# A pool for each operand slot with its splits four products later, the last two projection blocks written straight to the operands, and entry loads ordered by need

## The chip, the cores and the metric

The kernel runs on one core of a Trainium2 chip. The metric is the device time of one execution in microseconds (us), and a lower one is better. Times are the median of several runs; a profiled execution is a run of its own.

## The reference

One decoder layer over 1024 prompt rows and 64 sample rows (8 sequences of 8), 1088 rows in all, with a model width of 1024:

```python
# each layer: x += W_out . concat[NSA heads, multi-scale pooling channels](RMSNorm(x) @ W_in)
#             x += SwiGLU(RMSNorm(x)).   Final RMSNorm.
#   NSA heads: compressed-block, selected-block (top 16 of 64-token blocks) and
#              sliding-window branches, each a masked softmax, combined by gates
#   pooling channels: trailing means over 2/4/8/16 positions, a linear map per group
D_MODEL = 1024; SEQ = 1024; DEC_BATCH = 8; DEC_SEQ = 8; D_FF = 2816

def rms_norm(x, g):
    xf = x.astype(jnp.float32)
    y = xf * lax.rsqrt(jnp.mean(xf * xf, axis=-1, keepdims=True) + EPS)
    return (y * g.astype(jnp.float32)).astype(x.dtype)
```

Everything is fp32. The outputs are the new activations of prompt and sample rows and the rows to be written to the caches.

## The kernel before

**Numbers.** TensorE (PE) multiplies a 32-bit type of shorter mantissa, fp32r. So each fp32 operand is split in two: `hi` is a cast on ScalarE (ACT), `lo` is the rest, a subtraction on VectorE (DVE). A product is then three matmuls: hi·hi, hi·lo, lo·hi. The splits of PE's moving operand are `bhP1`…`bhP3` and `blP1`…`blP3` at the input products and the two halves of `r` at the output products; those of the weights are `sh` and `sl`, made of `wr` (raw) or `ws` (a sum or difference of raw ones).

**Stages.** Projections and compressed keys (to about 400 us of the profile); the attention stream; the entry of the feed-forward part; its input products; its output products; the last group of output products, with the final norm.

**The attention stream** works block by block of 128 queries (8 prompt blocks 0–7; the sample rows count as block 8). Softmax tiles `pcmp`, `psel`, `pwin` of a half block are scaled by 1/sum (`r`) on GpSimd (POOL, L1002), then transposed on PE (L1012) and split (L1020 on ACT, L1021 on DVE). Between its steps, `fill()` runs steps of other work: generators each with a rate, the steps per attention step. `RATES[0]` is the sample group, `RATES[1]` the pooling channels' part of the projection, `RATES[2]` the attention heads' part, `att_out`. What is left of `att_out` when the stream ends is run at the entry.

**att_out** takes blocks in the order 0, 1, 2, 7, 8, 6, 5, 4, 3. For each it loads the rows so far (`xr`) and the attention output (`of2`), splits the latter (`op0`, `op1`), and runs 48 matmuls (L1198–L1200) in two halves, each added to `xr` by DVE (L1272). Behind that, `xr` is stored as `x2t` (L1280), normed to `h`, and `h_out` transposes it (L1303) and multiplies by the norm's weight into `hT` (L1304), which is stored to DRAM: `hdA` for the half of rows of blocks 0, 1, 2, 7 and half of 8; `hdB` in three pieces (160, 128 and 128 rows) for half of 8 with block 6, block 5 and block 4. Block 3 is written to the operand tile itself.

**The entry** (`ffn`, L1478 on) takes four tiles `blk` as operand halves `hA` and `hB` and loads them from `hdA` and `hdB` on SP's queue, between the remaining fills. `combos` builds the seven operands of a Strassen-like scheme (P1, P2, P6, P5, P7, P4, P3, in that order) by subtractions (L1323) and splits (L163, L164). The input products are 22 units of 7 products, each of 24 matmuls of 128x272 (L1396). A product's result (`pq`, in PSUM) is taken out by ACT and DVE in `evict_in` (L1424–L1456), and the weight splits run four products ahead.

**The output products** are 3 groups of 4 units of 7 products of 18 matmuls. Their moving operands lie in DRAM (`td`) in fp32. A pool `ring` of seven tiles `r0`…`r6` holds the seven operands of a group. `load` takes a tile, starts its DMA on POOL's queue (L1565) and issues its split at once (`hilo`, ACT L1568, DVE L1569); the first seven are loaded ahead of the first group, and in the last unit of a group the product that was last to read a slot is followed by the load of that slot for the next group. Results are added to the rows `blk` by DVE (L1468), or copied by ACT in the first group (L1466). Two tiles `la0`, `la1` for the last group are loaded in unit 8.

**Memory.** A pool's memory is taken from what earlier pools freed; the first use of a tile waits for the last users of the memory under its whole pool. The memory under `ring` is that of the `b` tiles of the input products. DMAs on SP's queue are issued in order, and an issue that waits holds those behind it; POOL's queue holds DMA issues and POOL's own instructions alike. A scheduler sets the order on each engine by the order of the program and a priority.

## Time and profile before

| | before |
|---|---|
| median of 3 runs | 1445.89 us (1444.05 to 1447.25) |
| profiled execution | 1448.49 us, its span 1446.7 us |
| mean granted clock of PE | 0.978 |
| busy: PE, DVE, ACT, POOL | 1358.5 (94%), 980.2 (68%), 660.4 (46%), 200.0 (14%) us |
| DMA | 173.79 MB, 120 GB/s in the mean |

A row of the timeline has start and duration in us, then engine, line, operation, output and input tiles and shapes; in square brackets is the idle time of the engine just before, and what ended it. "SPq" and "POOL … DMA" rows are issues of transfers. A row of waits has the total in us, the number and the longest. `x2` or `(x2)` are instructions in the row. Durations of matmuls overlap, so distances between their starts say what each one costs.

### The profile page before, as it was taken

To read this page: it belongs to the slowest core of one execution; us is meant where nothing else is said; L and a number is where in the kernel's file an instruction comes from. 1 tells how busy PE (TensorE), PEld (TensorE's weight loads), DVE (VectorE), ACT (ScalarE), POOL (GpSimd) and SP (SyncE) were. 2 spreads that over 40 slices of the span, in tenths; PEclk is the share of its full clock that TensorE was granted. 3 is DMA by queue.
4 is the path that set the end of the run, shared out by engine and by line. 5 is a ranking of instruction groups with operands and counts; after the bars stand their busy time and mean duration, and the time that the engine had idled before them with its cause. 6 is when DMAs were issued, how large, how long until landed. Compare 5 with 4: busy or idle time off the path is not lost.

```text
span 1446.7 us, 25436 instructions
## 1 busy us (share of the span) xinstructions
PE 1358.5 (94%) x9490; PEld 1263.1 (87%) x9490; DVE 980.2 (68%) x2267; ACT 660.4 (46%) x1502; POOL 200.0 (14%) x338
## 2 busy tenths in 40 slices
PE   7979999899999989996799999999999989999995
PEld 6968999678878878775699999999999979999995
DVE  5655877777776688886866556655655565879557
ACT  7322554776566676764533333333333354434123
POOL 0124223422222232220000000000000010010000
PEclk9989999989999999998899999999999999999998
DMA  7457331534425143325232233333223262535135
GB/s 203 88 156 237 91 103 29 179 118 137 152 94 175 59 137 114 107 83 169 58 121 83 83 106 121 106 114 113 89 77 106 76 222 82 184 125 187 34 107 182
DMA packets 167751, 173.79 MB, mean 120 GB/s; under 512 B 21539, under 2 KB 134787, under 8 KB 166851
## 3 DMA queue, kind: packets, MB, share of 16 engines
q1 hardware_dynamic: 157187, 135.12, 30.5%
q0 software_dynamic: 9392, 35.45, 7.1%
q10 hardware_dynamic: 1048, 1.59, 1.0%
q8 instruction: 75, 1.23, 0.3%
q14 instruction: 49, 0.40, 0.1%
HBM read 113.87 MB, written 58.37 MB: 119 GB/s over the span
## 4 chain that ended last, share of the span: by engine, by line
PE 66%; issue 11%; DVE 9%; DMA 5%; ACT 4%; SPq 3%; POOL 1%; DVEq 0%; POOLq 0%; ACTq 0%
PE pq L1396 36%; PE dp L236 6%; PE tp L1012 3%; SPq L1060 3%; PE O L1036 2%; PE dp L1198 2%; PE dp L1200 2%; PE dp L1199 2%; PE O L1037 2%; PE S L923 2%; PE S L924 1%; DVE pl L1021 1%; DMA r<-td 1%; ACT ph L1020 1%; PE dp L1155 1%
## 5 line engine op out<-in xcount | busy, mean ns | idle before, releaser
L1396 PE MATMUL pq<-bhP,sh 128*128 128x272 f32 x1232 | 357.4, 290 | 11.5 <-ACT sh L163 5.7
L1396 PE MATMUL pq<-blP,sh 128*128 128x272 f32 x1232 | 357.4, 290 | 4.4 <-DVE blP L164 3.1
L1396 PE MATMUL pq<-bhP,sl 128*128 128x272 f32 x1232 | 355.3, 289 | 2.4 <-DVE sl L164 2.4
L1396 PEld LDWEIGHTS pq<-bhP,sh 128*128 128x128 f32 x1232 | 234.2, 190 | 13.3 <-ACT sh L163 6.5
L1396 PEld LDWEIGHTS pq<-blP,sh 128*128 128x128 f32 x1232 | 233.7, 190 | 5.5 <-DVE blP L164 5.5
L1396 PEld LDWEIGHTS pq<-bhP,sl 128*128 128x128 f32 x1232 | 233.6, 190 | 2.9 <-DVE sl L164 2.9
L1396 PE MATMUL pq<-r,sh 128*128 128x272 f32 x1008 | 194.4, 292 | 11.2 <-DVE blk L1468 5.7
L163 ACT CAST sh<-ws 128x512 fp32r<-128x512 f32 (+1 forms) x136 | 78.8, 583 | 217.5 <-PE pq L1396 153.2
L1396 PEld LDWEIGHTS pq<-r,sh 128*128 128x128 f32 x1008 | 160.4, 192 | 12.9 <-DVE blk L1468 6.0
L164 DVE TENSOR_TENSOR sl<-ws,sh 128x512 fp32r<-128x512 f32 (+1 forms) x136 | 86.7, 641 | 124.0 <-ACT sh L163 123.8
L1396 PE MATMUL pq<-r,sl 128*128 128x272 f32 x504 | 145.0, 289 | 0.0
L1021 DVE TENSOR_TENSOR pl<-tp,ph 128x512 fp32r<-128x512 f32 (+8 forms) x168 | 103.7, 622 | 42.6 <-ACT ph L1020 40.9
L163 ACT CAST sh<-wr 128x512 fp32r<-128x512 f32 (+1 forms) x102 | 59.3, 583 | 151.7 <-PE pq L1396 140.9
L1020 ACT CAST ph<-tp 128x512 fp32r<-128x512 f32 (+8 forms) x168 | 88.8, 534 | 67.5 <-PE tp L1012 60.7
L236 PE MATMUL dp<-h1h,whi 128*128 128x384 f32 (+1 forms) x336 | 112.9, 337 | 3.7 <-DVE ue L310 3.7
L236 PE MATMUL dp<-h1l,whi 128*128 128x384 f32 (+1 forms) x336 | 111.8, 333 | 0.0
L236 PE MATMUL dp<-h1h,wlo 128*128 128x384 f32 (+1 forms) x336 | 111.8, 333 | 0.0
L1565 POOL DMA_DIRECT2D r<-td x21 | 16.0, 765 | 631.5 <-PE pq L1396 625.6
L1396 PEld LDWEIGHTS pq<-r,sl 128*128 128x128 f32 x504 | 96.6, 192 | 0.0
L164 DVE TENSOR_TENSOR sl<-wr,sh 128x512 fp32r<-128x512 f32 (+1 forms) x102 | 65.0, 637 | 37.7 <-ACT sh L163 37.6
L1036 PE MATMUL O<-ph,vn 128*128 128x256 f32 x264 | 80.8, 320 | 3.2 <-DVE of L1047 1.7
L1002 POOL TENSOR_SCALAR pwin<-pwin,r 128x640 f32<-128x640 f32 (+4 forms) x64 | 42.7, 670 | 291.7 <-DVE r L995 144.9
(344 smaller groups left out, 3059.0 us busy)
## 6 DMA issues: line engine op xcount, KB each, us to landing
wr<-in_w_ffn_in SPq DMA_DIRECT2D x44, 512.0 KB
td<-blk SPq DMA_DIRECT2D x18, 1088.0 KB
r<-td POOLq DMA_DIRECT2D x21, 816.0 KB, 6.6
wr<-in_w_ffn_out SPq DMA_DIRECT2D x48, 192.0 KB
wraw<-in_w_in SPq DMA_DIRECT2D x14, 512.0 KB
x<-in_x_prompt SPq DMA_DIRECT2D x8, 512.0 KB
qi<-qd SPq DMA_DIRECT2D x8, 512.0 KB
op<-odp SPq DMA_DIRECT2D x16, 256.0 KB
```

The source lines that it names most:

```text
L163: nc.scalar.copy(hi, src)
L164: nc.vector.tensor_tensor(lo, src, hi.bitcast(F32), op=OP.subtract)
L236: nc.tensor.matmul(ps, w[:, k, :], x, start=(k == 0 and j == 0), stop=(k == kt - 1 and j == 2))
L923: nc.tensor.matmul(S[:, c0:c0 + n], q, kh[:, k0:k0 + n], start=True, stop=False)
L1002: nc.gpsimd.tensor_scalar(t, t, r[:, hh, b:b + 1], 1.0, op0=OP.mult, op1=OP.mult)
L1012: nc.tensor.transpose(tp[:kk, 256 * x + 128 * hh:256 * x + 128 * hh + 128], u["P"][hh, b][:, kb * 128:kb * 128 + kk], self.ident)
L1020: nc.scalar.copy(ph[:kk, a:e], tp[:kk, a:e])
L1021: nc.vector.tensor_tensor(pl[:kk, a:e], tp[:kk, a:e], ph[:kk, a:e].bitcast(F32), op=OP.subtract)
L1036: nc.tensor.matmul(o, vv, ph[:kk, cs], start=(2 * t + x == 0), stop=False)
L1037: nc.tensor.matmul(o, vv, pl[:kk, cs], start=False, stop=(2 * t + x == nb - 1))
L1060: reg = nc.sync.value_load(self.ptrow[0:1, 4 * b + kb:4 * b + kb + 1], min_val=0, max_val=39)
L1396: nc.tensor.matmul(ps[:, c, :HQ], w[:, k], x[:, k, cs], start=(fresh and k == 0 and j == 0), stop=(k == kt - 1 and j == 2), skip_group_che ...
```

## The change

It has five parts. `RATES[2]` goes from 1.7 to 1.3. The stores of `x2t`, `hdA` and `hdB` go from SP's to POOL's queue. Blocks 4 and 3 are both written straight to `hB` once that tile exists, so `hdB[2]` is neither stored nor loaded. The entry's loads are put in another order, with the weights' two halves apart. The ring becomes seven pools of one tile, and load and split are separated: the first seven loads are issued ahead of their seven splits, and later a split is issued four products behind its load.

```diff
--- before.py
+++ after.py
@@ -37,7 +37,7 @@
 LATE = (5, 4, 3)
 ORDER = ("P1", "P2", "P6", "P5", "P7", "P4", "P3")
 EPS = 1e-6
-RATES = (0.8, 0.65, 1.7)
+RATES = (0.8, 0.65, 1.3)
 BIG = 1e30
 HUGE = 3e38
 POOLW = (2, 4, 8, 16)
@@ -758,6 +758,7 @@
             self.pst = self.pool("pst2", 2, PSUM, stack=self.psy, side="right")
             self.os = self.ap.tile([128, 4, NS], F32, name="os", bufs=1)
             self.done, self.ofs = [], {8: self.os}
+            self.hB, self.direct = None, []
             self.fills, self.stage, self.hold = [], -1, False
             self.attn_stream()
         self.psx.close()
@@ -1277,7 +1278,7 @@
                     nxt = loads()
             for _ in self.tail:
                 yield
-            nc.sync.dma_start(self.x2t[j][:rows], x[:rows])
+            nc.gpsimd.dma_start(self.x2t[j][:rows], x[:rows])
             h = pool.tile([128, D], F32, name="h")
             ss = pool.tile([128, 1], F32, name="ss", bufs=2)
             v = pool.tile([128, 1], F32, name="v", bufs=2)
@@ -1291,8 +1292,11 @@
 
     def h_out(self, pool, j, rows, h):
         nc = self.nc
-        if j == 3:
-            hts = [b[:, :, 416:544] for b in self.hB]
+        direct = j in (3, 4) and self.hB is not None
+        if direct:
+            p0 = HOME[j][1]
+            hts = [b[:, :, p0:p0 + 128] for b in self.hB]
+            self.direct.append(j)
         else:
             hT = pool.tile([128, 8, 128], F32, name="hT")
             hts = [hT[:, 4 * q:4 * q + 4, :rows] for q in range(2)]
@@ -1307,14 +1311,14 @@
                 yield True
         if j in (0, 1, 2, 7):
             p0 = HOME[j][1]
-            nc.sync.dma_start(self.hdA[:, :, p0:p0 + 128], hT)
+            nc.gpsimd.dma_start(self.hdA[:, :, p0:p0 + 128], hT)
         elif j == 8:
-            nc.sync.dma_start(self.hdA[:, :, 512:544], hT[:, :, 0:32])
-            nc.sync.dma_start(self.hdB[0][:, :, 0:32], hT[:, :, 32:64])
+            nc.gpsimd.dma_start(self.hdA[:, :, 512:544], hT[:, :, 0:32])
+            nc.gpsimd.dma_start(self.hdB[0][:, :, 0:32], hT[:, :, 32:64])
         elif j == 6:
-            nc.sync.dma_start(self.hdB[0][:, :, 32:160], hT)
-        elif j != 3:
-            nc.sync.dma_start(self.hdB[6 - j], hT)
+            nc.gpsimd.dma_start(self.hdB[0][:, :, 32:160], hT)
+        elif not direct:
+            nc.gpsimd.dma_start(self.hdB[6 - j], hT)
         yield True
 
     def combos(self, hA, hB, B, a, e):
@@ -1333,6 +1337,10 @@
         put("P3", B1)
 
     def raw_w(self, u):
+        for _ in self.raw_parts(u):
+            pass
+
+    def raw_parts(self, u):
         if "raw" in u:
             return
         nc, fw, kt = self.nc, self.fw, u["kt"]
@@ -1345,6 +1353,7 @@
                 for e in range(2):
                     nc.sync.dma_start(r[:, e * kt:e * kt + kt], half[e])
             u["raw"].append(r)
+            yield
 
     def side_w(self, u, name):
         nc, fw, kt = self.nc, self.fw, u["kt"]
@@ -1483,14 +1492,23 @@
             B = {}
             ins = [dict(f=f, kt=4, B=B, evict=self.evict_in,
                         src=[(wsrc[:, :, o + 128 * f:o + 128 * f + 128],) for o in (0, FF)]) for f in range(NFF)]
-            for q in range(2):
-                nc.sync.dma_start(hA[q], self.hdA[:, 4 * q:4 * q + 4])
-            self.raw_w(ins[0])
+            pieces = ((0, 160), (160, 128), (288, 128))
+
+            def hb_load(i):
+                p0, n = pieces[i]
+                for q in range(2):
+                    nc.sync.dma_start(hB[q][:, :, p0:p0 + n], self.hdB[i][:, 4 * q:4 * q + 4])
+            w0 = self.raw_parts(ins[0])
+            nc.sync.dma_start(hA[0], self.hdA[:, 0:4])
+            next(w0)
+            nc.sync.dma_start(hA[1], self.hdA[:, 4:8])
+            hb_load(0)
             while self.fills:
                 self.fill()
-            for i, (p0, n) in enumerate(((0, 160), (160, 128), (288, 128))):
-                for q in range(2):
-                    nc.sync.dma_start(hB[q][:, :, p0:p0 + n], self.hdB[i][:, 4 * q:4 * q + 4])
+            hb_load(1)
+            next(w0)
+            if 4 not in self.direct:
+                hb_load(2)
             self.raw_w(ins[1])
             self.wax.close()
             att.close()
@@ -1521,7 +1539,7 @@
             last = self.pool("last", 1, stack=s, side="right")
             lacts = [last.tile([128, 2, 4, HT], F32R, name=f"la{j}") for j in range(2)]
             s4 = ExitStack()
-            ring = self.pool("ring", 1, stack=s4)
+            ring = [self.pool(f"ring{i}", 1, stack=s4) for i in range(7)]
             G, kt = 3, 3
             slot = dict(P1=0, P2=2, P3=3, P5=4, P6=5, P7=6, P4=7)
             Bs = [{} for _ in range(G)]
@@ -1532,11 +1550,13 @@
                 if not todo:
                     return
                 g, q = todo.pop(0)
-                r = ring.tile([128, 2, kt, HT], F32R, name=f"r{nr[0] % 7}")
+                r = ring[nr[0] % 7].tile([128, 2, kt, HT], F32R, name=f"r{nr[0] % 7}")
                 nr[0] += 1
-                Bs[g][q] = self.hilo(r, self.td[g][:, slot[q]].rearrange("k p n -> p k n"))
-            for _ in range(7):
-                load()
+                Bs[g][q] = r[:, 0], r[:, 1]
+                self.raw_in(r, self.td[g][:, slot[q]].rearrange("k p n -> p k n"))
+                return r
+            for r in [load() for _ in range(7)]:
+                self.hilo(r)
             outs = []
             for g in range(G):
                 rows = I["w_ffn_out"][0, 256 * kt * g:256 * kt * (g + 1)].rearrange("(j e p) c -> e p j c", e=2, p=128)
@@ -1544,12 +1564,18 @@
                     outs.append(dict(m=m, g=g, kt=kt, B=Bs[g], evict=self.evict_out,
                                      src=[[rows[e][:, :, 128 * mm:128 * mm + 128] for e in range(2)] for mm in (m, m + 4)]))
 
+            queue = []
+
             def hook(x, q):
-                if x % 4 == 3:
-                    load()
+                queue.append(load() if x % 4 == 3 and todo else None)
                 if x == 8 and q in ("P6", "P7"):
                     j = ("P6", "P7").index(q)
-                    self.hilo(lacts[j], self.tl[4 * j:4 * j + 4].rearrange("q p n -> p q n"), True)
+                    self.raw_in(lacts[j], self.tl[4 * j:4 * j + 4].rearrange("q p n -> p q n"))
+                    queue[-1] = lacts[j]
+                if len(queue) > 4:
+                    r = queue.pop(0)
+                    if r is not None:
+                        self.hilo(r)
             for _ in self.chains(self.sequence(len(outs)), outs, hook):
                 pass
             s4.close()
@@ -1558,16 +1584,15 @@
                     for f in range(4)]
             self.last_group(2 * kt * G, acts, s)
 
-    def hilo(self, r, src, late=False):
+    def raw_in(self, r, src):
+        self.tc.keep_in_program_order(self.nc.gpsimd.dma_start(r[:, 1].bitcast(F32), src))
+
+    def hilo(self, r):
         nc = self.nc
         hi, lo = r[:, 0], r[:, 1]
         raw = lo.bitcast(F32)
-        ld = nc.gpsimd.dma_start(raw, src)
-        if late:
-            self.tc.keep_in_program_order(ld)
         nc.scalar.copy(hi, raw)
         nc.vector.tensor_tensor(lo, raw, hi.bitcast(F32), op=OP.subtract)
-        return hi, lo
 
     def sequence(self, n, entry=False):
         seq = [(0, "P1"), (0, "P2")]
```

On SP's queue at the entry, before (`blk_8576` and `blk_8577` are the two halves of A, `blk_8578` and `blk_8579` those of B; `wr` are weights, `x2t3` block 3's rows):

```order
L1317 DMA hdB128_2_94<-hT_8609 128x1024
L1487 DMA blk_8576<-hdA_91 128x2176
L1487 DMA blk_8577<-hdA_91 128x2176
L1343 DMA wr_8585<-in_w_ffn_in 128x8x128
L1343 DMA wr_8587<-in_w_ffn_in 128x8x128
L1493 DMA blk_8578<-hdB160_0_92 128x4x160
L1280 DMA x2t3_85<-xr_8589 128x1024
L1493 DMA blk_8579<-hdB160_0_92 128x4x160
L1493 DMA blk_8578<-hdB128_1_93 128x4x128
L1493 DMA blk_8579<-hdB128_1_93 128x4x128
```

The same place after:

```order
L1502 DMA blk_8576<-hdA_91 128x2176
L1351 DMA wr_8584<-in_w_ffn_in 128x8x128
L1504 DMA blk_8577<-hdA_91 128x2176
L1500 DMA blk_8578<-hdB160_0_92 128x4x160
L1500 DMA blk_8579<-hdB160_0_92 128x4x160
L1500 DMA blk_8578<-hdB128_1_93 128x4x128
L1500 DMA blk_8579<-hdB128_1_93 128x4x128
L1351 DMA wr_8656<-in_w_ffn_in 128x8x128
```

The store of `hdB128_2` and its two loads are gone, `x2t3` is on another queue, and one weight row stands between the halves of A.

On POOL, the last scalings of the attention stream before:

```order
L1002 TENSOR_SCALAR pwin_8424<-pwin_8424,r_8426 128x512
L1002 TENSOR_SCALAR psel_8416<-psel_8416,r_8426 128x512
L1002 TENSOR_SCALAR pcmp_8396<-pcmp_8396,r_8426 128x32
L1002 TENSOR_SCALAR pwin_8477<-pwin_8477,r_8426 128x512
L1002 TENSOR_SCALAR psel_8460<-psel_8460,r_8426 128x512
L1002 TENSOR_SCALAR pcmp_8453<-pcmp_8453,r_8426 128x32
```

The same place after; `x2t4` is block 4's rows, `hdB128_1` block 5's transposed rows:

```order
L1003 TENSOR_SCALAR pwin_8384<-pwin_8384,r_8386 128x512
L1003 TENSOR_SCALAR psel_8376<-psel_8376,r_8386 128x512
L1003 TENSOR_SCALAR pcmp_8342<-pcmp_8342,r_8386 128x32
L1281 DMA x2t4_86<-xr_8172 128x1024
L1321 DMA hdB128_1_93<-hT_8351 128x1024
L1003 TENSOR_SCALAR pwin_8451<-pwin_8451,r_8386 128x512
L1003 TENSOR_SCALAR psel_8427<-psel_8427,r_8386 128x512
L1003 TENSOR_SCALAR pcmp_8420<-pcmp_8420,r_8386 128x32
```

Two stores stand ahead of the scalings of a half block; the same holds for the blocks ahead of these.

On DVE, the last input unit and the first operands of the output products, before (L1443 is the last step of a result, L1569 the split of an operand):

```order
L1357 TENSOR_TENSOR ws_13962<-ws_13960,wr_13838 128x384
L1443 TENSOR_TENSOR blk_13555<-g2_13651,u2_13702 128x544
L1569 TENSOR_TENSOR r0_13778<-r0_13778 128x1632
L1569 TENSOR_TENSOR r1_13782<-r1_13782 128x1632
L1569 TENSOR_TENSOR r2_13786<-r2_13786 128x1632
L164 TENSOR_TENSOR sl_13865<-wr_13838,sh_13864 128x384
L1468 TENSOR_TENSOR blk_13766<-pq3_13868,blk_13766 128x544
```

The same splits after (L1450 and L1452 are L1441 and L1443 of before, L1595 is L1569):

```order
L1366 TENSOR_TENSOR ws_13836<-ws_13834,wr_13820 128x384
L1595 TENSOR_TENSOR r0_13792<-r0_13792 128x1632
L1450 TENSOR_TENSOR g2_13424<-pq2_13432,g2_13424 128x544
L164 TENSOR_TENSOR sl_13587<-wr_13335,sh_13586 128x512
L1435 TENSOR_TENSOR g1_13521<-pq3_13590,g1_13521 128x544
L1452 TENSOR_TENSOR blk_13551<-g2_13424,u2_13485 128x544
L164 TENSOR_TENSOR sl_13620<-ws_13617,sh_13619 128x512
L1366 TENSOR_TENSOR ws_13846<-wr_13820,wr_13823 128x384
L164 TENSOR_TENSOR sl_13827<-wr_13820,sh_13826 128x384
```

The first split stands ahead of results of the unit before the last; all seven stood behind those of the last unit.

On DVE at the change to the second group, before:

```order
L1569 TENSOR_TENSOR r0_14344<-r0_14344 128x1632
L1468 TENSOR_TENSOR blk_13766<-pq3_14406,blk_13766 128x544
L164 TENSOR_TENSOR sl_14431<-wr_14198,sh_14430 128x384
L164 TENSOR_TENSOR sl_14460<-ws_14457,sh_14459 128x384
L1357 TENSOR_TENSOR ws_14569<-wr_14377,wr_14380 128x384
L164 TENSOR_TENSOR sl_14488<-wr_14377,sh_14487 128x384
L1569 TENSOR_TENSOR r1_14426<-r1_14426 128x1632
L1468 TENSOR_TENSOR blk_13769<-pq2_14324,blk_13769 128x544
L1569 TENSOR_TENSOR r2_14453<-r2_14453 128x1632
L164 TENSOR_TENSOR sl_14519<-ws_14516,sh_14518 128x384
L1569 TENSOR_TENSOR r3_14483<-r3_14483 128x1632
L1468 TENSOR_TENSOR blk_13766<-pq0_14522,blk_13766 128x544
```

The same place after (L1477 is L1468 of before):

```order
L1595 TENSOR_TENSOR r0_14358<-r0_14358 128x1632
L1477 TENSOR_TENSOR blk_13762<-pq3_14418,blk_13762 128x544
L164 TENSOR_TENSOR sl_14441<-wr_14212,sh_14440 128x384
L164 TENSOR_TENSOR sl_14470<-ws_14467,sh_14469 128x384
L1366 TENSOR_TENSOR ws_14577<-wr_14389,wr_14392 128x384
L164 TENSOR_TENSOR sl_14496<-wr_14389,sh_14495 128x384
L1477 TENSOR_TENSOR blk_13765<-pq2_14338,blk_13765 128x544
L164 TENSOR_TENSOR sl_14525<-ws_14522,sh_14524 128x384
L1595 TENSOR_TENSOR r1_14438<-r1_14438 128x1632
L1477 TENSOR_TENSOR blk_13762<-pq0_14528,blk_13762 128x544
L164 TENSOR_TENSOR sl_14551<-ws_14520,sh_14550 128x384
L1595 TENSOR_TENSOR r2_14463<-r2_14463 128x1632
```

The split of `r1` stands two rows further back and that of `r2` three; the additions that stood behind them, or between them, now stand ahead.

## The prediction

> **What bounds the kernel now.** I read the page's head, then busy time by stage, then the waits and the order of time around each stage in which TensorE (PE) is not full. The columns of a window row are us, then busy time of PE, its weight loads, VectorE (DVE), ScalarE (ACT) and GpSimd (POOL), then granted clock, share of the DMA engines and GB/s.
>
> ```profile
> span 1446.7 us, 25436 instructions
> 560.00:620.00 60.00, 59.77 (x351) 47.86 (x352) 48.56 (x176) 40.15 (x109) 12.37 (x20) 1.00 0.35 106
> 620.00:668.00 48.00, 42.19 (x256) 33.82 (x254) 36.89 (x133) 31.49 (x88) 12.38 (x24) 0.96 0.15 56
> 668.00:719.00 51.00, 32.60 (x176) 27.91 (x174) 40.53 (x52) 24.24 (x28) 0.00 (x0) 0.80 0.49 146
> 719.00:1158.00 439.00, 438.66 (x3500) 438.61 (x3501) 252.27 (x374) 151.26 (x253) 0.00 (x0) 1.00 0.32 100
> 1158.00:1190.00 32.00, 25.54 (x182) 24.55 (x181) 22.75 (x25) 18.13 (x22) 5.39 (x7) 0.89 0.66 243
> 1219.00:1286.00 67.00, 64.63 (x511) 64.16 (x510) 50.53 (x75) 27.36 (x41) 5.33 (x7) 1.00 0.42 135
> 1286.00:1373.00 87.00, 83.51 (x647) 82.83 (x646) 65.80 (x95) 30.29 (x42) 6.85 (x9) 0.98 0.41 133
> ```
>
> PE is full in 719–1158 (438.66 of 439), and nothing there can be won by order. It is not full in four places that the change touches: the end of attention, 620–668 (5.81 us idle); the entry of the feed-forward part, 668–719 (18.40 idle, and a clock of 0.80); the passage to the output products, 1158–1190 (6.46 idle, clock 0.89); and the two group changes in 1219–1286 and 1286–1373 (5.86 idle together, part of it beside them). Those are the most that can come out, some 36 us plus the lost clock.
>
> **Attention and the rate 1.7 → 1.3.** A step of the w_out fill issues matmuls like these, six rows from first to last:
>
> ```profile
> 610.37 0.39 PE L1198 MATMUL dp<-rwh,op 128*128 128x512 f32 x1
> ...
> 611.53 0.39 PE L1200 MATMUL dp<-rwh,op 128*128 128x512 f32 x1
> ```
>
> So one is 1.16/5 = 0.232 us of PE. By the order, when 880 of 1084 attention matmuls and transposes have been issued, 300 projection matmuls are out before and 254 after; both end at 324, as block 3 can only come at the entry. So 46 × 0.232 = 10.7 us of PE work, and with 16 transposes some 12.5 us, move from the stretch up to 620, where PE has 0.23 us of 60 free, to 620–668, where 5.81 are free. Work that leaves a full stretch shortens it by all of itself and comes back later, so the sum is not changed by the move; what it wins is bubbles filled, at most 5.8 us. But DVE too gets work there (added rows, squares' tail, transposes' copies), and it has 11.1 us free. From +3 (DVE makes PE wait) to −5 (nearly all bubbles filled); I take **−2**, nearer the middle, since 3 of the 5.8 us are waits for DVE or ACT that more independent matmuls can cover.
>
> **The entry.** In order of time, what stands between the last attention work and the full stream:
>
> ```profile
> 668.18 0.68 DVE L164 TENSOR_TENSOR op<-of,op 128x512 fp32r<-128x512 f32 x1
> 668.30 0.32 SPq L1317 DMA_DIRECT2D hdB<-hT  x1
> 668.95 0.97 SPq L1487 DMA_DIRECT2D blk<-hdA  x2
> 673.74 4.09 SPq L1493 DMA_DIRECT2D blk<-hdB  x1
> 675.46 2.00 ACT L163 CAST bhP<-blk 128x2176 fp32r<-128x2176 f32 x1 [7.86 <-DMA blk<-hdA]
> 677.50 2.43 DVE L164 TENSOR_TENSOR blP<-blk,bhP 128x2176 fp32r<-128x2176 f32 x1 [1.44 <-ACT bhP L163]
> 680.98 0.59 PE L1396 MATMUL pq<-bhP,sh 128*128 128x272 f32 x1 [5.65 <-ACT sh L163]
> 687.73 1.89 DVE L1323 TENSOR_TENSOR blk<-blk 128x1664 f32<-128x1664 f32 x1 [0.87 <-DMA blk<-hdB]
> 710.74 0.60 PE L1396 MATMUL pq<-bhP,sh 128*128 128x272 f32 x1 [2.18 <-ACT bhP L163]
> 715.09 0.68 DVE L164 TENSOR_TENSOR blP<-blk,bhP 128x512 fp32r<-128x512 f32 x1
> 719.34 0.39 PE L1396 MATMUL pq<-bhP,sh 128*128 128x272 f32 x1 [0.70 <-ACT g L1430]
> 680.00:684.00 4.00, 1.66 (x4) 1.07 (x4) 3.84 (x9) 1.45 (x3) 0.00 (x0) 0.50 1.11 351
> 710.00:714.00 4.00, 1.78 (x6) 1.47 (x7) 4.00 (x6) 1.21 (x3) 0.00 (x0) 0.50 0.00 0
> 691.00:719.00 28.00, 18.00 (x109) 15.98 (x107) 27.20 (x29) 15.78 (x19) 0.00 (x0) 0.82 0.05 13
> ```
>
> Before, SP first stores block 4's rows (0.5 MB at 668.30), then issues both A loads behind it; A0 lands at 675.46, 7.86 us after ACT had nothing else; DVE's list of subtractions and splits starts at 677.50 and ends with 715.09 + 0.68 = 715.77; the stream is whole from 719.34. In 691–719 DVE is busy 27.20 of 28: here the list on DVE sets the end, and every us by which it starts earlier, or stands still less, comes out. The change removes the 0.5 MB store and its two loads of 0.25 MB, puts A0 alone ahead, then one weight row, A1, B. A0's load waits for the last split of block 3's operand (668.18), which now stands ahead of the two transposed copies; it can go at about 668.3 rather than 668.95. The 680–684 row shows 351 GB/s at a DMA share of 1.11, so the entry's transfers run one after another at that rate: 0.5 MB less ahead is 1.4–1.5 us, and A0 (1.1 MB) with nothing beside it takes 3.2 us and its start. I get A0 at 673.3 (−2.1). DVE's list begins at 675.4 rather than 677.5, its waits for B (0.87 us at 687.73 and 1.4 us at its start) go, and as it is 33–34 us long it ends near 709.2 against 715.77: −6.5. PE's own wait of 5.65 us at 680.98 becomes 3–4. The stretch then ends 4.6–6 us earlier, less about 1 for a clock that can stay at 0.50 longer when PE is fed in bits: **−5**. The ends are −2 (A0 earlier only, the list otherwise as it is) and −7 (all of the list's gain).
>
> Block 4's rows written to the operands cost the same DVE instruction as before with another target; hidden or not, it counts 0. The x2t store of block 3 leaves SP's queue (0.5 MB, on POOL's now) and no longer stands between the two B loads; its bytes still share the engines, which is in the ends.
>
> The 680–684 row has clock 0.50 behind the wait of 5.65 us. The Trainium skill, "TensorE: Matmul & The Clock Gate", Part 1, has the half clock after an idle window of about 3.4 us; by that rule an entry wait shortened below 3.4 us would keep full clock and win 2 us more, which is an estimate of that page alone and not in the sum. The 710–714 row speaks against it: 0.50 again, and the waits there are 2.18 and shorter.
>
> **The passage to the output products.**
>
> ```profile
> 1159.68 0.39 PE L1396 MATMUL pq<-bhP,sh 128*128 128x272 f32 x1 [0.99 <-ACT u L1433]
> 1163.26 5.40 POOL L1565 DMA_DIRECT2D r<-td  x7 [502.84 <-PE pq L1396]
> 1168.52 1.55 ACT L1568 CAST r<-r 128x1632 fp32r<-128x1632 f32 x1 [1.10 <-DMA r<-td]
> 1170.12 0.59 PE L1396 MATMUL pq<-r,sh 128*128 128x272 f32 x1 [4.15 <-ACT r L1568]
> 1172.01 0.59 PE L1396 MATMUL pq<-r,sh 128*128 128x272 f32 x1 [1.30 <-DVE r L1569]
> 1170.00:1174.00 4.00, 2.58 (x10) 2.27 (x11) 3.35 (x2) 1.63 (x3) 0.00 (x0) 0.50 1.00 357
> 1176.15 0.61 ACT L1466 COPY blk<-pq 128x544 f32<-128x544 f32 x1 [0.60 <-PE pq L1396]
> ...
> 1219.76 0.76 POOL L1565 DMA_DIRECT2D r<-td  x1 [51.10 <-PE pq L1396]
> 1224.68 1.55 ACT L1568 CAST r<-r 128x1632 fp32r<-128x1632 f32 x1 [0.22 <-DMA r<-td]
> ```
>
> Before, all seven operand loads wait for one event at 1163.26: the last reader of the memory of the b tiles, because one pool of seven tiles is freed memory to be taken as a whole. Then the load, ACT's cast and DVE's subtraction follow in a chain, and PE waits 4.15 and 1.30 us and works at half clock in 1170–1174 (4 us that are worth 2) until about 1177. With seven pools, slot 0 waits only for P1's tile, whose last reader is P1 of the last unit; by the order eight products are issued behind that one ahead of the event, and a product takes 2.85 us (the 439 us of the stage hold 154), so slot 0 can be loaded from about 1163.3 − 22.8 = 1140.5. A load lands 4.9 us after its issue (1219.76 to 1224.68). Its splits are 1.55 on ACT and 1.86 on DVE, done 15 us ahead of use. The last slot, on P4's tile, is loaded about when it was, but its product is the sixth of the unit, some 14 us later. What goes: 4.15 + 1.30 + about 2 of lost clock = 7.4; what comes: ACT's queue holds a cast that waits for a landing, ahead of the copy that releases P4 of the last unit; that wait, 0.99 at 1159.68, may become 0.7–2.2. Net **−6.2**, ends −3.5 (three us of new waits in ACT's and DVE's queue) and −8.5 (also the 0.99 gone).
>
> **The two group changes.**
>
> ```profile
> PE pq L1396 <- DVE blk L1468: 5.7, 4, 3.0
> 1226.27 1.86 DVE L1569 TENSOR_TENSOR r<-r 128x1632 fp32r<-128x1632 f32 x1 [1.05 <-ACT r L1568]
> 1316.00:1320.00 4.00, 1.04 (x5) 1.04 (x6) 4.00 (x6) 2.53 (x3) 0.00 (x0) 0.90 0.58 204
> ```
>
> Four waits of PE, 5.7 us, are for DVE's addition of a result (L1468), which frees the accumulator. It is late since the seven splits of 1.86 us stand ahead of it in DVE's queue: DVE is full (4.00 of 4). The change puts each split four products later, behind the additions. One unit is 7 products of 18 matmuls, 15.9 us of PE at 0.126 us each; DVE has 7 × 1.8 = 12.5 us of splits and 10.2 of its own per unit, 22.7, so over one unit it is still short by 7 us, over two it has 9 to spare. Each split is needed only three products after its new place, and the backlog is then paid in time that PE doesn't wait for. I take 80% of 5.7 plus the lost clock: **−4.7**, ends −1 (the waits turn from the addition to the split itself) and −7.
>
> **POOL's queue**, on which the 17 stores now go:
>
> ```profile
> L1565 POOL DMA_DIRECT2D r<-td x21 | 16.0, 765 | 631.5 <-PE pq L1396 625.6
> 658.79 0.69 POOL L1002 TENSOR_SCALAR pwin<-pwin,r 128x512 f32<-128x512 f32 x1 [1.31 <-DVE r L995]
> PE tp L1012 <- POOL pwin L1002: 0.8, 2, 0.6
> SPq L1280 <- DVE xr L1272: 26.2, 5, 12.6
> ```
>
> A store takes POOL 0.765 us. It stands ahead of the scalings of a half block, on which PE's transposes wait; PE waited for them 0.8 us in all in 520–668. POOL is 12–14 us busy of 40–60, and the rows that the stores wait for are made ahead of the scaling's own operand on DVE, but for the last two pairs. So I count 0 for it, with +1 at one end; without that cover two stores cost 1.53 us a block, the rival below. SP's waits for the same rows (26.2 us) go, and SP has no late load behind them at the entry but those counted.
>
> The SBUF page of the Trainium skill ("SBUF — State Buffer", the trap in which DVE blocks DMA) has a transfer from POOL's queue go from about 620 to 3100 ns beside a copying DVE; as an estimate by that page alone 17 stores would hold POOL for 40 us more. The trace's 765 ns, in a stage with DVE busy 50.53 of 67, don't show that; the page itself names copies, not additions of two tensors.
>
> **The sum**: −2 −5 −6.2 −4.7 = −17.9, rounded down to −17 as a wait that goes seldom goes whole. The profiled execution took 1448.49 us (span 1446.7), 2.6 above the median 1445.89 of the runs; 1445.89 − 17 = **1429**.
>
> **Rivals.** A: attention or the entry gives its part back (the tail becomes DVE's: 12 us of DVE's work into 11.1 free; or the entry's DVE list is as long as before): +3 −2 −6.2 −4.7 = −9.9, with the same rounding −8: **1438**. For it: DVE 27.20 of 28. B, slower: POOL's queue. If each pair of stores delays the scalings in full, 8 pairs × 1.53 = 12 us; if a store of 1024 rows of 128 elements takes longer in proportion to its rows (the loads' 384 rows 0.77, so 2.05), a pair is 2.82 and 8 are 22.6: 1445.89 − 17 + 22.6 = **1452**. It decides from about 2.1 us a pair exposed. Against it: PE's 0.8 us of waits. C: the early loads hold ACT's queue in the last units so that the passage wins nothing and the group changes a half: −2 −5 −2.4: **1436**. D: the pools still wait for a common event and the delays move nothing: attention and entry cancel, **1445**.
>
> **Chances.** Forecast 0.60, A 0.14, C 0.09 (these make faster), D 0.07, B 0.10. What a measurement can tell from no change here is 0.2%, 2.9 us. Faster 0.83, same 0.07, slower 0.10. The terms' ends sum to −27 and −3; not all meet, so the range is from 1419 (the entry, the passage and the groups near their ends) to 1441 (A with one more end); B and D lie above it.
>
> **What would show it.** Right: A0's cast starts before 674 and the stream is whole by 715; no wait of PE over 2 us for slot 0 after the last input unit, and clock 1.00 there; the wait row for L1468 under 1.5 us. Wrong: PE waits for POOL's scalings of several us before the entry; a store on POOL of over 1.5 us; PE's waits for a split (L1595) in place of the additions; the entry ending with DVE busy and no earlier than 718.

## The result and the profile after

The changed kernel takes 1428.79 us in the median of 4 runs (1427.47 to 1430.67) against 1446.57 for the one before in the same comparison. The ratio is 0.9874 with a 95% interval of [0.9846, 0.9903]. A second comparison of the same two, with more runs of both, gave 1429.58 against 1446.27, and 0.9873 [0.9852, 0.9893]. The forecast was 1429. The sum held; two of its terms, attention's and that of POOL's queue, did not, and they cancelled.

First the head of the page and the stretches of the profile after that answer to those of before. The columns are those of the prediction's window rows; the stretches begin where the same work begins.

```profile
span 1425.7 us, 25457 instructions
661.00:711.00 50.00, 35.74 (x193) 31.33 (x194) 42.91 (x56) 25.83 (x31) 0.58 (x1) 0.84 0.45 136
711.00:1145.00 434.00, 433.30 (x3453) 433.09 (x3453) 251.23 (x372) 150.61 (x250) 2.47 (x4) 1.00 0.33 103
1145.00:1165.00 20.00, 18.38 (x147) 18.16 (x146) 15.61 (x15) 14.11 (x16) 2.79 (x4) 1.00 0.76 283
1203.00:1266.00 63.00, 60.98 (x485) 60.79 (x485) 48.93 (x72) 26.18 (x39) 5.25 (x7) 1.00 0.45 144
1266.00:1352.00 86.00, 84.79 (x668) 83.99 (x667) 66.68 (x97) 31.35 (x44) 6.74 (x9) 1.00 0.41 135
```

The passage (1145–1165) now has PE busy 18.38 of 20 at full clock, where 1158–1190 before had 25.54 of 32 at 0.89. The group changes lack 2.02 and 1.21 us instead of 2.37 and 3.49, and the second no longer loses clock. The entry still has 14.26 us of 50 idle and a clock of 0.84.

To say where the time went, each kernel's trace is cut at the same five events: the sixth last copy of an attention output by ACT (`otmp`), the start of DVE's last `of`, the fifth copy of `g` in the input products, the tenth copy of a `blk` in the output products, and the first cast of `lh` in the last group. Their starts before are 525.75, 666.10, 741.21, 1213.03 and 1372.92; after, they are 521.41, 659.62, 732.30, 1196.56 and 1351.26. The lengths between them give this table (us, against the profile before):

| kernel | median | ratio, 95% interval | start | attention's end | entry | input products, passage | group changes | last group |
|---|---|---|---|---|---|---|---|---|
| changed | 1428.79 | 0.9874 [0.9846, 0.9903] | −4.3 | −2.1 | −2.4 | −7.6 | −5.2 | +0.7 |
| changed again | 1429.58 | 0.9873 [0.9852, 0.9893] | −0.2 | −0.9 | −1.4 | −7.6 | −5.6 | −0.4 |
| rate alone | 1441.17 | 0.9969 [0.9955, 0.9982] | −2.3 | −6.2 | −0.6 | +0.5 | +1.0 | −0.8 |
| ring alone | 1433.92 | 0.991 [0.9889, 0.9931] | +0.4 | 0.0 | 0.0 | −7.5 | −6.7 | 0.0 |
| entry alone | 1443.2 | 0.9985 [0.9971, 1.0] | −2.2 | +1.6 | −5.2 | −0.3 | +0.2 | 0.0 |
| stores alone | 1446.66 | 1.0005 [0.9991, 1.002] | −1.6 | −0.6 | −2.1 | +0.6 | +0.5 | −0.1 |
| pools, no delay | 1439.23 | 0.9948 [0.9928, 0.9968] | −0.8 | −0.8 | −0.7 | −5.5 | −1.7 | +0.3 |
| delay, one pool | 1440.76 | 0.9954 [0.9939, 0.9969] | +0.1 | +1.0 | −0.2 | −0.2 | −5.5 | +0.2 |
| changed, stores on SP | 1421.43 | 0.9832 [0.9809, 0.9854] | −0.6 | −5.5 | −5.6 | −7.7 | −7.2 | −0.4 |
| changed, 3 stores on SP | 1421.98 | 0.9839 [0.9816, 0.9861] | −2.0 | −5.8 | −5.4 | −7.7 | −5.8 | −0.7 |
| stores on SP, 1 on POOL | 1422.02 | 0.9827 [0.9805, 0.985] | −2.8 | −5.8 | −1.8 | −7.6 | −6.5 | +1.3 |
| stores on SP, rate 1.5 | 1426.44 | 0.9858 [0.9833, 0.9883] | −1.3 | −0.1 | −5.5 | −7.7 | −6.9 | +0.5 |
| stores on SP, rate 1.15 | 1422.4 | 0.9836 [0.9814, 0.9859] | −3.3 | −5.8 | −4.3 | −7.1 | −7.0 | +1.4 |

A stage that a kernel does not touch shows how far one profiled execution can be trusted: mostly within 1 us, at the worst 1.6 (attention's end of "entry alone"). The start is the same instructions on PE in all of them, and yet spans 4.7 us; it is told of at the end. (Some of the expectations below call the first event the fifth last output; it is the sixth last.)

### The profile page after: what moved, and what is told of

Its sections match the earlier page's. It is cut to its first block, busy times and chain, and to the rows that moved or that the text cites. A ratio compares the mean times of both kernels' runs of the same rounds, so it can differ in the third digit from the quotient of the medians.

```text
span 1425.7 us, 25457 instructions
## 1 busy us (share of the span) xinstructions
PE 1350.0 (95%) x9490; PEld 1261.4 (88%) x9490; DVE 976.0 (68%) x2267; ACT 659.6 (46%) x1502; POOL 209.5 (15%) x355
## 4 chain that ended last, share of the span: by engine, by line
PE 70%; DVE 8%; issue 8%; DMA 5%; SPq 4%; ACT 4%; POOL 1%; DVEq 0%; POOLq 0%; ACTq 0%
PE pq L1405 38%; PE dp L236 7%; PE tp L1013 4%; SPq L1061 3%; PE O L1037 2%; PE dp L1199 2%; PE dp L1201 2%; PE O L1038 2%; PE dp L1200 2%; PE S L924 2%; PE S L925 2%; DMA r<-td 1%; DVE blP L164 1%; PE dp L1156 1%; DVE pl L1022 1%
## 5 line engine op out<-in xcount | busy, mean ns | idle before, releaser
L1405 PE MATMUL pq<-r,sh 128*128 128x272 f32 x1008 | 191.0, 289 | 3.2 <-DVE blk L1477 3.2
```

The costliest lines, as they stand in the source:

```text
L1405: nc.tensor.matmul(ps[:, c, :HQ], w[:, k], x[:, k, cs], start=(fresh and k == 0 and j == 0), stop=(k == kt - 1 and j == 2), skip_group_che ...
```

## The experiments

**The parts, one at a time.** Four kernels, each the one before with one part of the diff:

```diff
-RATES = (0.8, 0.65, 1.7)
+RATES = (0.8, 0.65, 1.3)
```

> The kernel before with one number changed, RATES[2] 1.7 to 1.3. Theory 1 (the deferred projection work fills bubbles of PE at the end of attention): from the last but five output blocks of attention to the entry 2 us less, the entry as before, 1443 to 1445. Theory 2 (the 2 us of that stretch came from the stores' leaving SP's queue, not from the rate): within 0.5 us of before. Theory 3 (a lower rate alone pushes work to the entry): slower by 1 to 3 us.

Measured 1441.17, ratio 0.9969 [0.9955, 0.9982]: 4.5 us faster, and 6.2 us shorter at the end of attention. All three theories had too small a size or the wrong sign. The rate is the whole of attention's gain, and it is three times the forecast's 2. The stretch from the sixth last output to the end of attention, before and with the rate alone:

```profile
525.75:666.10 140.35, 133.00 (x787) 106.93 (x788) 113.54 (x399) 95.11 (x260) 34.46 (x57) 0.99 0.30 98
523.48:657.65 134.17, 128.92 (x787) 106.90 (x788) 111.29 (x401) 95.39 (x260) 34.33 (x57) 0.99 0.31 102
```

PE's idle time falls from 7.35 to 5.25 us, so 2.1 of the 6.2 are idle time that was filled. The other 4.1 are PE's busy time: the same 787 matmuls keep it busy for 133.00 us and for 128.92, at the same clock. What shortens them no run here shows.

```diff
-            ring = self.pool("ring", 1, stack=s4)
+            ring = [self.pool(f"ring{i}", 1, stack=s4) for i in range(7)]
...
-                Bs[g][q] = self.hilo(r, self.td[g][:, slot[q]].rearrange("k p n -> p k n"))
+                Bs[g][q] = r[:, 0], r[:, 1]
+                self.raw_in(r, self.td[g][:, slot[q]].rearrange("k p n -> p k n"))
...
+                if len(queue) > 4:
+                    r = queue.pop(0)
+                    if r is not None:
+                        self.hilo(r)
```

> The kernel before with the ring's part alone: seven pools, loads apart from splits, splits four products later. Theory 1: the passage to the output products wins 7.5 us and the group changes 4.5, so 12 less, 1433 to 1435, and all stages ahead of 1130 us as before. Rival: the early loads and casts win only where the entry left DVE and ACT in another phase, so 6 to 8 less.

Measured 1433.92: 12 us less, as theory 1 has it. Nothing moves ahead of the passage. The two stages sum to −14.2 in the profile.

```diff
-        if j == 3:
+        direct = j in (3, 4) and self.hB is not None
...
+            nc.sync.dma_start(hA[0], self.hdA[:, 0:4])
+            next(w0)
+            nc.sync.dma_start(hA[1], self.hdA[:, 4:8])
+            hb_load(0)
```

> The kernel before with the entry's part alone: blocks 4 and 3 written to the operand tiles, no third piece of hdB in DRAM, loads in the new order; stores stay on SP's queue, rate 1.7. Theory 1: 2.4 us less between the last attention output and the full stream of the input products, 1443 to 1445. Rival (the entry's gain needs the stores off SP's queue, as the last of them holds the first A load): under 1 us. Second rival (the forecast's term): 5 less.

Measured 1443.2, 0.9985 [0.9971, 1.0]: 2.2 us by the ratio, its interval from 4.2 to none. That fits theory 1. In the profile the entry alone is 5.2 us shorter, the size of the forecast's term, and twice what the changed kernel shows; attention's end is 1.6 longer there. The runs' interval leaves out 5.2, so this kernel by itself does not settle what the edit is worth. Four kernels further down, whose entry is also 4.3 to 5.6 us shorter, speak for the profile, and then something else in the changed kernel takes half of it back.

```diff
-            nc.sync.dma_start(self.x2t[j][:rows], x[:rows])
+            nc.gpsimd.dma_start(self.x2t[j][:rows], x[:rows])
# and the same for the five lines that store hdA and hdB
```

> The kernel before with the 17 stores on POOL's queue alone. Theory 1: no loss at the scalings, as each store costs POOL 0.5 to 0.9 us and its data is there ahead of the scaling's; within 1 us of before, or 1 us less where SP's queue is freer. Rival (SP's waits of 26 us for those rows held loads that attention needed): 2 to 3 us less by the entry. Second rival (POOL's queue holds the scalings): 3 or more us slower, with PE's waits for POOL several us.

Measured 1446.66 against 1446.03, ratio 1.0005 [0.9991, 1.002]: no difference beside the rate and the entry of before, as theory 1 has it. (It has 18 stores on POOL, not 17, as with the entry of before block 4's rows of `hdB` are stored too.)

**Pools and delay apart.** The ring's part again, with the queue emptied at once, and with one pool:

```diff
-                if len(queue) > 4:
+                if len(queue) > 0:
```

> The kernel before with seven pools and the first seven loads ahead of their splits, but every later split issued at once behind its load. Theory 1 (the pools make the passage, the delay makes the group changes): 7.5 us less at the passage, nothing at the two group changes, 1438 to 1439. Rival (the pools also free the group changes, as a load waits for one slot's reader alone): 10 or more less, with waits of PE for DVE's additions under 3 us.

```diff
-            ring = [self.pool(f"ring{i}", 1, stack=s4) for i in range(7)]
+            ring = self.pool("ring", 1, stack=s4)
...
-                r = ring[nr[0] % 7].tile([128, 2, kt, HT], F32R, name=f"r{nr[0] % 7}")
+                r = ring.tile([128, 2, kt, HT], F32R, name=f"r{nr[0] % 7}")
```

> The kernel before with the splits four products behind their loads, but one pool for all seven slots. Theory 1: 4.5 to 6.5 us less at the group changes and nothing at the passage, which still waits for one event, 1439 to 1442. Rival (the passage wins from loads that are issued ahead of all splits even in one pool): 2 us more won there.

The waits of PE from the last input units on, in us in total, number and longest, first with pools and no delay, then with the delay and one pool:

```profile
PE pq L1396 <- DVE blk L1468: 6.2, 6, 2.0
PE pq L1396 <- ACT u L1433: 2.1, 1, 2.1
```

```profile
PE pq L1396 <- ACT r L1576: 4.1, 1, 4.1
PE pq L1396 <- DVE blk L1468: 2.0, 3, 0.7
PE pq L1396 <- DVE r L1577: 1.3, 1, 1.3
```

Pools take the waits for the first operand away and leave 6.2 us for DVE's additions; the delay does the reverse, and keeps the 4.1 and 1.3 us of before at the passage. The times, 1439.23 and 1440.76, are those that theory 1 gives, and both gains are nearly additive in the ring's −12. By stage the pools alone win 5.5 us at the passage, where the whole ring wins 7.5: behind the wait of 2.1 us for `u` their clock is 0.77 and 0.80 in 1158–1166, while it stays at 1.00 in the ring's trace behind one of 1.7.

**What took the entry's and attention's gain back.** The rate alone had −6.2 at attention's end and the changed kernel −2.1, or −0.9 in its second profile. Just ahead of the end of attention its trace has PE's longest wait of the whole stretch. ACT, DVE, POOL and PE of the changed kernel:

```profile
650.92 1.15 ACT L1289 ACTIVATE h<-xr,r 128x1024 f32<-128x1024 f32 x1 [3.44 <-DVE r L258]
651.97 1.05 ACT L1021 CAST ph<-tp 128x512 fp32r<-128x512 f32 x2
647.88 1.29 DVE L256 SCALAR_TENSOR_TENSOR t<-r,v 128x1 f32<-128x1 f32 x1
...
650.66 0.16 DVE L258 TENSOR_TENSOR r<-r,t 128x1 f32<-128x1 f32 x1
645.66 0.60 POOL L1281 DMA_DIRECT2D x2t<-xr  x1 [0.99 <-DVE xr L1273]
647.23 0.53 POOL L1321 DMA_DIRECT2D hdB<-hT  x1 [0.98 <-DVE r L996]
647.80 0.70 POOL L1003 TENSOR_SCALAR pwin<-pwin,r 128x512 f32<-128x512 f32 x1
652.59 0.58 PE L1037 MATMUL O<-ph,vn 128*128 128x256 f32 x1 [3.14 <-ACT ph L1021]
652.00:656.00 4.00, 3.27 (x14) 2.97 (x15) 1.98 (x3) 1.65 (x5) 0.00 (x0) 0.50 0.00 0
```

ACT waits 3.44 us for `r`, the end of DVE's chain of small steps for block 4's norm, and only then casts `ph`, for which PE waits 3.14 us; the clock is 0.50 in 652–656 behind it. The second profile has the same two waits, 3.44 and 3.1 us. With the rate alone, ACT at the same place reads:

```profile
651.00 1.07 ACT L1020 CAST ph<-tp 128x512 fp32r<-128x512 f32 x2 [1.31 <-PE tp L1012]
653.05 0.59 ACT L1020 CAST ph<-tp 128x512 fp32r<-128x512 f32 x1 [0.98 <-PE tp L1012]
653.53 1.15 ACT L1288 ACTIVATE h<-xr,r 128x1024 f32<-128x1024 f32 x1
```

There three of the casts (the first row has two) stand ahead of the norm's scaling (L1288), and the scaling waits for nothing. The diff changes none of these instructions; only their order is another. A second piece of order differs at the entry: in the changed kernel three casts of weights (`sh`) stand behind all casts of the B operands (`bhP`), and in other kernels ahead of them or among them. The stores decide both, as the next kernels show. Which store moves the first piece was not run alone: block 5's `hdB` rows, or block 4's `x2t`.

```diff
 # the changed kernel, with all its stores back:
-            nc.gpsimd.dma_start(self.x2t[j][:rows], x[:rows])
+            nc.sync.dma_start(self.x2t[j][:rows], x[:rows])
```

> The changed kernel with the 17 stores put back on SP's queue. In the changed kernel's trace PE stands 3.1 us at 649.4 and then works at half clock, since ACT has the norm's scaling of block 4's rows (L1289) ahead of three casts and that scaling waits 3.4 us for DVE's chain; with the rate alone the scaling stands behind the casts, and by the order it does so here again. Theory 1 (the stores on POOL's queue cause this order and so cost 4 us): the stretch from attention's fifth last output to its end is 6 us shorter than before the change instead of 2.1, and the time is 4 us below the changed kernel's, 1423 to 1426. Rival (the entry needs the stores off SP's queue, as block 3's store stands between loads): the 4 us are given back at the entry, within 1 us of the changed kernel.

> The changed kernel once more, as the measure beside which the one with its stores on SP's queue is read: 1427 to 1431 in the median. Theory 1 (the stretch ahead of 380 us, the same instructions in all kernels, differs by up to 4 us from run to run): its start of the fifth last attention output lies at 521 to 526 us, and from there to the end it is 16 to 17 us shorter than before. Rival (the change itself wins 4 us ahead of that point): 521 again.

Measured 1421.43 beside 1429.58 of the changed kernel: 8 us faster, twice what theory 1 gives, since the entry too gains 3 to 4 us instead of giving any back. The ratios to the kernel before, 0.9832 [0.9809, 0.9854] and 0.9873 [0.9852, 0.9893], overlap by a hair; the 5 runs of the one and the 6 of the other do not overlap at all (1420.05 to 1424.82, and 1425.13 to 1432.47). The second profile of the changed kernel also answers its own expectation: its start is 525.58, so the 4.3 us won there in the first profile are not the change's, and from there on it is 15.9 us shorter than before. The version with its stores on SP's queue is the fastest measured here.

That left open whether POOL's time or the order is at fault. Two kernels tell them apart:

```diff
+            (nc.sync if j in (3, 4) else nc.gpsimd).dma_start(self.x2t[j][:rows], x[:rows])
...
         elif not direct:
+            nc.sync.dma_start(self.hdB[6 - j], hT)
```

> The changed kernel with three of its 17 stores back on SP's queue: the rows x2t of blocks 4 and 3, and the transposed rows of block 5; the other 14 stay on POOL. By the order, ACT's queue then stands as with all stores on SP: the norm's scaling of block 4 behind three casts, and two weight casts at the entry ahead of the B operands' casts. Theory 1 (the loss of the stores on POOL is these two pieces of order, not POOL's time): the time is that of the kernel with all stores on SP, 1420 to 1424. Rival (14 more DMAs on POOL hold its scalings, some 0.3 to 0.6 us each): 1425 to 1429.

```diff
+            (nc.gpsimd if j == 3 else nc.sync).dma_start(self.x2t[j][:rows], x[:rows])
 # all other stores on nc.sync
```

> The changed kernel with 16 stores on SP's queue and one on POOL's, the rows x2t of block 3, which is behind all of POOL's scalings. By the order only the entry then stands as in the changed kernel: two weight casts on ACT behind the casts of the B operands. Theory 1 (this place of two weight casts costs the entry some 3 us): attention as with all stores on SP (5.5 us less than before the change), the entry 2 to 2.5 us less instead of 5.5, so 1424 to 1425. Rival (with block 3's store off SP's queue the last B load goes earlier): faster than with all on SP, under 1421.

With 14 of 17 stores still on POOL the time is 1421.98, and attention's end and the entry are as short as with none there. So POOL's queue as such costs nothing, as the forecast said. The three stores moved back take with them their own time on POOL, too, but in the changed kernel's rows that is little: block 5's store ends at 647.76 and the scaling behind it starts at 647.80, 0.6 us after its operand `r` was there (647.21), while ACT waits 3.44 for another engine. The loss is the order's. With the one store on POOL that comes behind all of POOL's scalings, attention keeps its −5.8 and the entry falls from −5.4 to −1.8. But its median, 1422.02, lies between theory 1's 1424 and the rival's 1421 and does not show the 3.6 us of the profile. Its runs (1419.88 to 1425.24) are like those of the other two kernels, and the profiled one is the slowest of its five. So this half rests on the traces: the three profiles with that order at the entry have −1.4 to −2.4, the five with the entry's edits and the other order −4.3 to −5.6. By the runs the first piece of order may cost the whole 8 us, by the traces it costs half of it; which is right stays open. The entry of both, from DVE's last `of` to the fifth copy of `g`, PE's waits ahead of the product P7 of the first unit, and the stretch from that product's start to the next one's, first with three stores on SP, then with one on POOL:

```profile
658.27:727.96 69.69, 55.13 (x353) 50.62 (x352) 55.57 (x76) 33.83 (x45) 0.00 (x0) 0.90 0.39 117
705.20 0.39 PE L1405 MATMUL pq<-bhP,sh 128*128 128x272 f32 x1 [0.73 <-ACT g L1439]
705.20:709.18 3.98, 3.28 (x24) 3.06 (x24) 3.65 (x7) 1.32 (x3) 0.00 (x0) 1.00 0.46 132
```

```profile
657.54:730.83 73.29, 58.08 (x353) 53.34 (x352) 55.80 (x76) 33.94 (x45) 0.64 (x1) 0.86 0.37 112
704.87 0.59 PE L1405 MATMUL pq<-bhP,sh 128*128 128x272 f32 x1 [1.42 <-ACT sh L163]
706.03 0.59 PE L1405 MATMUL pq<-bhP,sl 128*128 128x272 f32 x1 [0.34 <-DVE sl L164]
704.87:712.08 7.21, 6.17 (x24) 5.53 (x25) 4.76 (x9) 2.41 (x5) 0.00 (x0) 0.53 0.53 145
```

PE is idle some 15 us in both (14.56 and 15.21). The difference is the clock, 0.90 against 0.86: in the second kernel PE waits 1.42 us for a cast of a weight ahead of P7, and that product of 24 matmuls takes 7.21 us at a clock of 0.53; in the first the weight is there, and the product takes 3.98 us at 1.00. That is 3.2 of the 3.6 us.

**The rate.**

> The changed kernel with all stores on SP's queue and RATES[2] 1.5 instead of 1.3. Theory 1 (the lower rate wins by filling the attention's end, where PE stands 5.8 us before the change): half of that is won, so the stretch from the fifth last output to the end of attention is 2 to 4 us shorter than before the change, 1422 to 1425. Rival (what counts is that the last full stretch holds less projection work, and any rate under 1.7 that still ends in time does the same): 1421, as with 1.3.

> The same with RATES[2] 1.15. Theory 1 (the end of attention has no more bubbles to fill at 1.3, so what is deferred further comes back one for one or stands open at the entry): 1421 to 1426. Rival (more to win by deferring more): under 1420.

At 1.5 attention's end gains nothing (−0.1), at 1.15 the same as at 1.3 (−5.8), with a little given back at the entry; the medians are 1426.44 and 1422.4. So the gain is not in proportion to what is deferred. Theory 1 holds for 1.15; for 1.5 it falls, as does its rival. With all stores on SP's queue, PE is busy throughout the full stretch at 1.3 and not at 1.5, first the rows of 1.3, then of 1.5:

```profile
563.00:590.00 27.00, 27.00 (x171) 22.95 (x170) 23.14 (x86) 20.34 (x57) 7.87 (x12) 1.00 0.32 102
590.00:620.00 30.00, 30.00 (x191) 24.55 (x190) 25.27 (x98) 21.75 (x59) 6.94 (x12) 1.00 0.34 94
```

```profile
564.00:598.00 34.00, 33.15 (x200) 26.51 (x199) 28.45 (x97) 22.82 (x65) 7.39 (x12) 1.00 0.32 105
598.00:630.00 32.00, 31.21 (x193) 25.50 (x192) 27.05 (x101) 22.14 (x59) 6.95 (x12) 1.00 0.41 115
```

These stalls are 1.6 us of the 5.4 by which the two kernels differ at attention's end; the rest is again busy time, 133.3 us against 129.6 for the same 787 matmuls. What stalls PE at 1.5 was not followed further. It stays open whether it is the amount of work or again a piece of order.

## Why the prediction was right, and where it was not

**Attention, forecast −2, measured −2.1 and −0.9.** The number is right, by luck. With the rate alone the fourth of the last six outputs comes 10.1 us earlier, against 10.7 us of deferred matmuls, and about 4 of these are given back by the end. The mechanism told, idle time of PE that is filled, is there and has the size that was taken: 2.1 us with the rate alone. But the rate wins 6.2 in all, more than the 5.8 of idle time that were to be the most. The step that failed is that only filled bubbles count: 4.1 us more come from a shorter busy time of the same matmuls, for which no run here shows the cause; that a rate of 1.5 wins nothing doesn't follow from filled bubbles either. Then 3.7 to 5 us (against the −5.8 of two kernels above) are lost to the order of ACT's queue. Two errors cancelled.

**The entry, forecast −5, measured −2.4 and −1.4.** The term was that of the entry's edits, and alone they give −5.2 in the profile (2.2 by the runs). Two steps failed. One is the sentence that DVE's list sets the end and that every us by which it ends earlier comes out: against the last `of`, the list ends 4.1 us earlier (706.36 instead of 716.97, with the 6.5 us of attention's end taken off; the prediction's 715.77 is the last split but one), and PE gets 2.4 of it. With three stores on SP the list ends only 3.4 us earlier by that count, and the entry wins 5.4. The other is the list's length of 33–34 us: it was 39.5 before, with DVE busy for 36.4 of them, and is 36.7 now. The loads did as said, A0's cast starting 1.4 us earlier by the same count (forecast 2.1). The us that went missing are PE's own, at half clock behind waits for a weight's cast:

```profile
706.47 0.59 PE L1405 MATMUL pq<-bhP,sh 128*128 128x272 f32 x1 [1.41 <-ACT sh L163]
706.00:710.00 4.00, 3.20 (x12) 2.88 (x13) 4.00 (x8) 1.56 (x3) 0.00 (x0) 0.50 0.42 124
713.55 0.39 PE L1405 MATMUL pq<-bhP,sh 128*128 128x272 f32 x1 [0.70 <-ACT u L1442]
```

Of the signs that were named, A0's cast before 674 came in both profiles of the changed kernel (667.60 and 672.96). The full stream by 715 came in the first (713.55), whose start was 4.3 us early, and not in the second (719.99).

**The passage, forecast −6.2, measured −7.1 to −7.7 in every kernel with the seven pools and the delay.** Mechanism and size were right. The wait that was to come, for `u` behind a cast in ACT's queue, was there (1.62 us at 1152.40, forecast 0.7 to 2.2); no wait for slot 0 is left, and the first load goes at 1132.05, which with the 8.9 us won so far is 1141 on before's scale (forecast 1140.5, from a product of 2.85 us; the products of the full stream start 3.01 us apart):

```profile
1132.05 0.78 POOL L1588 DMA_DIRECT2D r<-td  x1 [462.15 <-PE pq L1405]
1152.40 0.39 PE L1405 MATMUL pq<-bhP,sh 128*128 128x272 f32 x1 [1.62 <-ACT u L1442]
1160.03 0.60 ACT L1475 COPY blk<-pq 128x544 f32<-128x544 f32 x1
```

**The group changes, forecast −4.7, measured −5.2 and −5.6.** The waits for additions fell from 5.7 to 3.2, not under the 1.5 that the forecast named, and the clock that was 0.98 in 1286–1373 is 1.00; the ring alone leaves 2.1 and wins 6.7. The mechanism was right, as the delay alone wins 5.5. That DVE has 9 us to spare over two units was not: by the prediction's own figures two units hold the seven splits and twice DVE's own 10.2, 32.9 us in 31.8 of PE. At the first change PE still waits 2.0 us for an addition.

```profile
PE pq L1405 <- DVE blk L1477: 3.2, 4, 2.0
```

**POOL's queue, forecast 0, cost some 8.** This is the step that failed most dearly. All its reasons hold as far as they go: a store took POOL 0.53 to 0.94 us, PE's waits for the scalings are 1.0 us, and 14 stores on POOL cost nothing that can be measured. What it did not look at is that the edit also moves instructions on an engine that it does not name: ACT's scaling ahead of three casts, with the wait of 3.14 us and the half clock behind it. The rival B, 1452, had the loss on the right edit by the wrong way, and far too large. The 40 us that the prediction works out beside it from the Trainium skill's page "SBUF — State Buffer" did not occur.

**The sum.** −2.1 −2.4 −7.6 −5.2 with +0.7 in the last group is −16.6 for the profiled execution, and the forecast's rounded −17 was for these. The other 4.3 us by which the two profiles differ lie ahead of 525 us and are not the change's, as the second profile of the changed kernel shows. (Rival A's −9.9, rounded in the same way, is −9, so 1437 and not 1438; nothing hangs on it.)

## What to carry to other kernels

Where a scheduler sets the order, an edit that moves a DMA to another queue can move compute on engines that it doesn't name: after such an edit, compare the order on every engine at the places where PE waits, above all which in-order queue now holds an instruction that waits ahead of one that PE needs. A reload into memory that another pool frees should be a pool for each slot, and a split that follows a load in an in-order queue belongs as many products behind it as its use allows; here each is worth 5 to 7 us by itself. A total that agrees with its forecast does not show that the terms do: run the parts alone.

## What the runs showed of the hardware

The stretch ahead of 525 us differs by up to 4.7 us between profiled executions with the same instructions in the same order on PE. The granted clock differs there, in one 40 us stretch as follows, before and after:

```profile
300.00:340.00 40.00, 37.21 (x214) 30.95 (x214) 28.26 (x108) 23.84 (x74) 12.75 (x26) 0.87 0.49 152
300.00:340.00 40.00, 37.37 (x233) 31.41 (x231) 30.53 (x120) 25.99 (x82) 13.03 (x27) 0.96 0.51 158
```

So 0.87 and 0.96, with PE busy alike; at 0.87 fewer matmuls are done in it (214 and 233). This stretch alone does not make the difference: the second profile of the changed kernel has 0.96 there too, and starts at 525.58. A part's gain is better read from its own stage than from two spans.

The half clock does not need one long wait. In the changed kernel it comes at 706–710 (0.50), where no wait in the 12 us ahead is over 1.6 us but PE is busy only 5.93 of them:

```profile
694.00:698.00 4.00, 1.20 (x7) 0.79 (x6) 4.00 (x3) 1.36 (x1) 0.00 (x0) 1.00 0.00 0
698.00:702.00 4.00, 2.83 (x21) 2.39 (x19) 4.00 (x5) 2.62 (x3) 0.00 (x0) 1.00 0.00 0
702.00:706.00 4.00, 1.90 (x12) 1.47 (x12) 4.00 (x7) 1.34 (x3) 0.00 (x0) 0.97 0.01 4
```

The Trainium skill, "TensorE: Matmul & The Clock Gate", Part 1, has the gate watch how busy PE has been, and gives half rate after an idle window of about 3.4 us; these rows agree with the first, and here the half clock came with no such idle window.

A DVE step of one column (L256) that takes 0.22 us at 649.59 and 650.22 took 1.29 at 647.88, beside two scalings on POOL, from 647.80 to 649.15; it ends at 649.17. It reads two tiles. The Trainium skill, "SBUF — State Buffer", section "Who interferes with whom", has a DVE instruction with two inputs in SBUF contend with a POOL instruction that reads SBUF; this row agrees. It is 1.07 us of the 3.44 that ACT waits for that chain.
